# Rows of y in freed weight slots, a list entry from two wide comparisons, the next router's weights in the middle of the expert stage, splits and loads ahead of the branch

## The chip, the cores and the metric

One core of a Trainium2 chip runs the whole program: TensorE (PE), VectorE (DVE), ScalarE (ACT), GpSimd (POOL) and SyncE (SP), which issues most DMAs, in the order written for its queue. The metric is device microseconds of one execution, the median of several.

## The reference

Two decoder layers over 1024 tokens of width 1024, in float32. Layer 0 mixes tokens with a causal convolution module, layer 1 with HGRN2 (a gated linear recurrence, 8 heads of 128). After either mixer comes a hierarchical mixture of experts:

```python
grp_val, grp_idx = top1(softmax(h @ grp_w + grp_b))        # 4 groups
top_val, top_idx = top2(logits of the 8 experts of that group)
gate = grp_val * softmax(top_val)                          # two (token, expert) pairs a token
y = (silu(x @ w_gate[e]) * (x @ w_up[e])) @ w_down[e]      # blocks of at most 128 rows of one expert
h = h + sum of the token's two y, each times its gate
```

There are 32 experts with three matrices of 1024 x 512, 6 MB for one expert. Each sublayer takes its input through an RMS norm, and a last norm ends the trunk.

## The kernel before

Every float32 matmul is made of three: an operand is split into a high half (ScalarE copies it into the matmul format, `wh`) and a low half (VectorE subtracts, `wl`), and high x high, low x high, high x low are summed in PSUM (lines 228 to 240, 680 to 694).

**The expert stage** (`moe`, lines 521 to 946) runs twice. The router's last part (`route`, lines 366 to 455) makes on VectorE a table `tidx` of the rows of each expert; `counts` (line 607) and lines 798 to 801 make `nvt`, the number of further blocks of 128 rows that experts with over 128 rows need. All engines load it and take a branch (lines 802 and 803). Its body (lines 804 to 826) loops over blocks beyond those planned, and is skipped on these inputs. Behind it stand 32 blocks, one an expert, and in layer 0 one listed block more. A block needs six chunks of weights of 1 MB (gate, up, down, two each), each split in two halves; a half is prepared three halves ahead of its matmuls (`prepare`, line 780), over four buffers. Chunks go round twelve slots in layer 0: four of `ring`, two of `ring3`, two of `ring4`, four of `keep`. The first eight are loaded before the stage, the others when a slot is free, in SP's order. A block's rows are gathered by GpSimd (`gather`, line 665), turned on TensorE and split (`x_T`), and its results scattered to `yD` (line 670). The last expert's rows stay on the chip: a one-hot matrix `place` (`places_of`, line 945) spreads them over the tokens with a matmul (`with_last`, line 954).

The extra block of layer 0 is listed on the chip: `entry` (line 733) compares the place of every pair with the block's first place, tile by tile: sixteen compares on VectorE into two buffers of 128 x 128, and a small matmul behind each (lines 744 to 749). It is called after block 19 of the loop, and its sums are read by lines 554 to 566.

**The order.** The instructions of one basic block are ordered for each engine by a planner that simulates a timeline; an instruction may be placed well ahead of where it is written, when its operands are free. `InOrder` keeps the order of TensorE, VectorE and ScalarE for the instructions inside it. `tc.issue_after(x)` lets what it holds stand behind x on x's engine, without a wait. So `places_of`, written at the end of the stage, and `load_router(1)`, written after it, ran ahead of the first branch.

**From the experts to HGRN** (lines 1259 to 1318). `fetch` loads h (8 tiles) into the slots of `keep`, two tiles of y into `ring`, and the first two chunks of HGRN's input weights. `read0` reads the two y rows of 128 tokens (1 MB). For each of eight tiles: y's two rows are added (tile 0 on VectorE, the others on GpSimd, line 1304), h and the last expert's rows are summed in PSUM (`with_last`), VectorE adds y, the norm follows, and TensorE turns the tile and the halves are split (`rows_T`). Tiles 2 to 7 of y go into four buffers `my`, whose memory comes free when the expert stage ends; so tiles 6 and 7 wait until tiles 2 and 3 have been turned. Then come the projections of head 0 (`proj_T` for q and f, by halves of the tokens, and `proj_rows`, by tiles), and the heads one after the other: while one head's recurrence runs, the next one's projections fill TensorE.

Of the kernel before, what the change touches and what calls it, by code (L numbers as in the profile page):

```python
# [13 lines left out]
OP = mybir.AluOpType  # L14
# [25 lines left out]
YB = 4  # L40
# [19 lines left out]
YDVE = (0,)  # L60
# [19 lines left out]
def trunk(ctx, tc, x, conv_norm_w, conv_pw1_w, conv_pw1_b, conv_dw_w, conv_dw_b, conv_ln_g, conv_ln_b,  # L80
# [27 lines left out]
    wides = [None]  # L108

    def load_w(ap3, pool=None):  # L110
        t = (pool or ring).tile([P, WIDE if pool is wides[0] else 2048], F32, name="wraw")[:, :2048]
        v = t if len(ap3.shape) == 2 else t.rearrange("p (a b) -> p a b", a=ap3.shape[1])
        nc.sync.dma_start(v, ap3)
        return t
# [56 lines left out]
    def load_router(l):  # L171
# [10 lines left out]
        nc.vector.tensor_tensor(rw, rw, fcol[:, :, None].to_broadcast([P, KD, 36]), op=OP.mult)  # L182
        r = {"rw": rw, "rb": rb, "lg": const.tile([P, NT, 36], F32, name="lgall"),
# [44 lines left out]
    def split_half(pool, raw, i):  # L228

        hi = pool.tile([P, 1024], F32R, name="wh", bufs=WB)  # L230
        lo = pool.tile([P, 1024], F32R, name="wl", bufs=WB)
# [5 lines left out]
    def split(pool, raw):  # L237

        for i in range(2):
            yield split_half(pool, raw, i)  # L240
# [280 lines left out]
    def moe(l, router, raws, slots, after, last=None, kept=None):  # L521
# [3 lines left out]
        with ExitStack() as held:  # L525
# [6 lines left out]
            over = ring2  # L532
# [163 lines left out]
            def mm_in(ps, xt, raw, c):  # L696
                for z, w in enumerate(split(mp, raw)):
                    done = mm_half(ps, xt, w, 4 * c + 2 * z)
                return done
# [24 lines left out]
            def mm_down(pd, ht, raw, c):  # L724
                for z, w in enumerate(split(mp, raw)):
                    mm_down_half(pd, ht, w, 2 * c + z)

# [5 lines left out]
            def entry(i, tag):  # L733
# [10 lines left out]
                for s in range(2):  # L744
                    for j in range(NT):
                        pl1 = mp.tile([P, P], BF, name="pl1")
                        nc.vector.tensor_scalar(pl1, iota_r, rel[:, s, j:j + 1], None, op0=OP.is_equal)
                        nc.tensor.matmul(tb[:, 0:6], pl1, qv[:, s, j], start=(s == 0 and j == 0),
# [31 lines left out]
            def prepare(n):  # L780
                if n >= len(seq):
                    return
# [4 lines left out]
                with inorder:  # L787
                    ready[n] = split_half(mp, raw_of[key], z)

            gather(xgs[0], cols(0)[0])  # L790
            gather(xgs[1], cols(1)[0])

# [8 lines left out]
            nc.vector.tensor_copy(nvt, nvf)  # L801
            nv = nc.values_load(nvt[0:1, 0:1], min_val=0, max_val=NOV)
            with tc.If(nv > nb - NE):
# [4 lines left out]
                list_rest()  # L808
                with tc.For_i(nb - NE, nv, 1) as it:
# [7 lines left out]
                    for c in range(2):  # L817
                        mm_in(opg, oxt, load_w(moe_src(l, ev, 'g', c), over), c)
                    for c in range(2):
                        mm_in(opu, oxt, load_w(moe_src(l, ev, 'u', c), over), c)  # L820
                    oht = h_T2(h_T(opg, opu))
                    opd = pp.tile([P, D], F32, name="pd", bufs=3 - PGB)
                    for c in range(2):
                        mm_down(opd, oht, load_w(moe_src(l, ev, 'd', c), over), c)
# [24 lines left out]
            for n, (i, part, c, z) in enumerate(seq):  # L849
# [48 lines left out]
                if s_ == 11 or (i == 0 and s_ == 7):  # L898
# [3 lines left out]
                    if i == 4 and l == 0:  # L902
# [4 lines left out]
                                     pp.tile([P, 16], F32, name="tp"))  # L907
                    if i == 20 and nb > NE:
# [16 lines left out]
            left = after(mp)  # L925
# [50 lines left out]
    ring3 = apool("ring30", 2)  # L976
    ring4 = apool("ring40", 2)
    wides[0] = ring4
    with tc.tile_pool(name="convo", bufs=1) as co_pool:
# [10 lines left out]
        with tc.tile_pool(name="a1", bufs=2) as ap, tc.tile_pool(name="a1ps", bufs=2, space=PSUM) as pp:  # L990
# [144 lines left out]
            for n, c in enumerate(ORDER):  # L1135
                if n == 3:
                    router = load_router(0)
# [571 lines left out]
```

## Time and profile before

| | |
|---|---|
| median of three runs | 2361.22 us (2357.2 to 2363.15) |
| profiled execution | 2353.6 us, of which the span 2351.8 |
| PE, DVE, ACT, POOL busy | 95%, 78%, 62%, 22% of the span |
| DMA in the expert stages | some 380 GB/s, share near 1.00 |
| expert stage of layer 0 | about 452 to 1067 us |
| HGRN | about 1067 to 1700 us |
| expert stage of layer 1 | about 1733 to 2320 us |

The page's strip of granted TensorE clock reads 9 in most of its 40 slices and less around 440 us, 1060 us and 1720 us: there one stage gives way to the next. TensorE's busy share of 95% is a mean over stages; the idle time lies in few places. A tile's name in the trace is that of the program (`wl<-wraw,wh`), and "L234" is line 234 of the kernel before.

### The profile page before, as it was taken

How to read it: one execution, taken by the hardware profiler on the slowest of the kernel's cores; microseconds unless marked ns; L12 is line 12 of the kernel's file. 1: busy time of each engine (PE TensorE's matmuls, PEld its weight loads, DVE VectorE, ACT ScalarE, POOL GpSimd, SP SyncE). 2: the span in 40 equal slices, each digit the busy share in tenths (PEclk: the TensorE clock that was granted, in tenths of full speed). 3: DMA queues.
4: the chain of work that ended last, by engine and by line, in shares of the span. 5: the costliest groups of instructions: out<-in, count | busy, mean ns of one | idle time of the engine just before them, and what ended most of it. 6: DMA issues, size and time to landing. Idle time of an engine off the chain costs nothing. (4 is left out here: it accounts for less than half of the span.)

```text
span 2351.8 us, 31895 instructions
## 1 busy us (share of the span) xinstructions
PE 2226.2 (95%) x11825; PEld 1863.3 (79%) x11825; DVE 1842.5 (78%) x2517; ACT 1458.1 (62%) x2035; POOL 511.8 (22%) x310
## 2 busy tenths in 40 slices
PE   7999899699999999998899999989979999999997
PEld 5888777578888878875899999977758888888885
DVE  5898656599999989997376666673479999999996
ACT  5654245378888878884334343332348888888884
POOL 1997301322111111103000000020051111111104
PEclk9999899799999999999999999989979999999999
DMA  5212424499999999987202020205259999999985
GB/s 169 72 55 73 135 90 144 154 338 359 373 377 373 394 354 388 397 323 252 72 14 77 10 82 26 65 32 208 84 201 366 378 374 384 392 391 398 383 329 230
DMA packets 138019, 547.68 MB, mean 233 GB/s; under 512 B 28969, under 2 KB 61921, under 8 KB 87936
## 3 DMA queue, kind: packets, MB, share of 16 engines
q1 hardware_dynamic: 116720, 504.22, 57.5%
q0 software_dynamic: 18720, 33.60, 3.9%
q10 hardware_dynamic: 2416, 7.75, 0.9%
q8 instruction: 95, 1.56, 0.3%
q14 instruction: 68, 0.56, 0.1%
HBM read 519.66 MB, written 60.42 MB: 247 GB/s over the span
## 5 line engine op out<-in xcount | busy, mean ns | idle before, releaser
L234 DVE TENSOR_TENSOR wl<-wraw,wh 128x1024 fp32r<-128x1024 f32 x780 | 932.7, 1229 | 80.6 <-ACT wh L233 71.1
L233 ACT ACTIVATE wh<-wraw 128x1024 fp32r<-128x1024 f32 x780 | 804.3, 1056 | 93.2 <-PE pd L722 77.3
L692 PE MATMUL pu<-wh,xh 128*128 128x512 f32 x520 | 214.6, 413 | 0.0
L692 PE MATMUL pg<-wh,xh 128*128 128x512 f32 x520 | 210.6, 405 | 2.1 <-ACT xh L270 2.1
L692 PE MATMUL pg<-wl,xh 128*128 128x512 f32 x520 | 207.0, 398 | 2.4 <-DVE wl L234 2.2
L692 PE MATMUL pg<-wh,xl 128*128 128x512 f32 x520 | 206.2, 397 | 2.0 <-DVE xl L271 1.9
L720 PE MATMUL pd<-wh,hth 128*128 128x512 f32 x520 | 205.2, 395 | 2.7 <-ACT hth L270 2.7
L692 PE MATMUL pu<-wh,xl 128*128 128x512 f32 x520 | 205.5, 395 | 0.0
L721 PE MATMUL pd<-wl,hth 128*128 128x512 f32 x520 | 204.8, 394 | 0.8 <-DVE wl L234 0.6
L722 PE MATMUL pd<-wh,htl 128*128 128x512 f32 x520 | 204.4, 393 | 0.8 <-DVE htl L271 0.8
L692 PE MATMUL pu<-wl,xh 128*128 128x512 f32 x520 | 203.9, 392 | 0.0
L666 POOL DMA_INDIRECT xg<-xD,tidx x64 | 99.8, 1560 | 463.7 <-PE tp L314 417.5
L671 POOL DMA_INDIRECT yD<-y,yidx x64 | 82.9, 1295 | 497.9 <-ACT y L730 490.2
L1074 POOL TENSOR_TENSOR wraw<-wraw,tap 128x1024 f32<-128x1024 f32 x60 | 155.0, 2584 | 40.5 <-ACT tap L1073 36.1
L1365 PE MATMUL pa<-wih,xh 128*128 128x256 f32 x512 | 147.8, 289 | 5.8 <-ACT q L1346 4.5
L1365 PE MATMUL pa<-wil,xh 128*128 128x256 f32 x512 | 147.6, 288 | 0.0
L1365 PE MATMUL pa<-wih,xl 128*128 128x256 f32 x512 | 147.5, 288 | 0.0
L270 ACT ACTIVATE xh<-tp 128x512 fp32r<-128x512 f32 x146 | 87.0, 598 | 74.3 <-PE tp L314 74.1
L692 PEld LDWEIGHTS pg<-wl,xh 128*128 128x128 f32 x520 | 99.2, 191 | 25.1 <-DVE wl L234 6.8
L692 PEld LDWEIGHTS pg<-wh,xl 128*128 128x128 f32 x520 | 98.8, 190 | 24.3 <-DVE xl L271 3.8
L720 PEld LDWEIGHTS pd<-wh,hth 128*128 128x128 f32 x520 | 98.6, 190 | 23.9 <-ACT hth L270 3.5
L721 PEld LDWEIGHTS pd<-wl,hth 128*128 128x128 f32 x520 | 98.5, 190 | 23.8 <-DVE wl L234 3.0
(492 smaller groups left out, 4874.5 us busy)
## 6 DMA issues: line engine op xcount, KB each, us to landing
wraw<-in_moe_w_gate_dram SPq DMA_DIRECT2D x130, 1024.0 KB, 7.5
wraw<-in_moe_w_up_dram SPq DMA_DIRECT2D x130, 1024.0 KB, 7.6
wraw<-in_moe_w_down_dram SPq DMA_DIRECT2D x130, 1024.0 KB, 7.4
wraw<-in_hgrn_w_in_dram SPq DMA_DIRECT2D x16, 1024.0 KB, 6.6
wraw<-in_conv_pw_w_dram SPq DMA_DIRECT2D x12, 1024.0 KB, 7.0
wraw<-yD SPq DMA_DIRECT2D x10, 1024.0 KB, 9.1
xD<-xn SPq DMA_DIRECT2D x16, 512.0 KB, 2.6
my<-yD SPq DMA_DIRECT2D x6, 1024.0 KB, 6.5
```

The source lines that it names most:

```text
L233: nc.scalar.activation(hi, r, AF.Copy)
L234: nc.vector.tensor_tensor(lo, r, hi, op=OP.subtract)
L270: turned[1] = nc.scalar.activation(hi, ps, AF.Copy)
L666: return nc.gpsimd.indirect_dma_start(out=xg, out_offset=None, in_=xD[l][:, :], in_offset=bass.IndirectOffsetOnAxis(ap=idx, axis=0), bound ...
L671: s = nc.gpsimd.indirect_dma_start(out=yD[l][:, :], out_offset=bass.IndirectOffsetOnAxis(ap=idx, axis=0), in_=y, in_offset=None, bounds_ch ...
L692: done = nc.tensor.matmul(ps, x_[:, kk + k], w_[:, k], start=(kk + k == 0 and x_ is xh and w_ is wh), stop=(kk + k == KD - 1 and x_ is xl))
L720: nc.tensor.matmul(pd[:, ns], hh[:, kk], wh[:, ns], start=(kk == 0), stop=False)
L721: nc.tensor.matmul(pd[:, ns], hh[:, kk], wl[:, ns], start=False, stop=False)
L722: turned[0] = nc.tensor.matmul(pd[:, ns], hl[:, kk], wh[:, ns], start=False, stop=(kk == KF - 1))
L1074: nc.gpsimd.tensor_tensor(res[c], res[c], t, op=OP.add)
L1365: nc.tensor.matmul(pa[:, :256], x_[:, k, js], w_[:, k].rearrange("p z c -> p (z c)"), start=(k == 0 and w_ is wh and x_ is xh), stop=(k == ...
```

## The change

- `entry`: for each of the two slots one compare makes the one-hot rows of all eight tiles (one buffer of 128 x 8 x 128); the sixteen matmuls stay.
- `load_router` is cut in two. `router_weights(1)` (five DMAs and the scaling of `rw`) is written behind block 15's end in the first expert stage, behind the last load on SP.
- The first two halves are split in two steps: `split_hi` (ScalarE) ahead of the count and the branch, `split_lo` (VectorE) behind it, around the turning of the first rows.
- In layer 0 the four loads that follow the first eight are issued ahead of the branch, each waiting for `nvt`.
- `after` (`fetch`, `places_of`) stands, on VectorE, behind the last split of hidden rows.
- `ring3` and `ring4` lie on the other side of the memory and live until HGRN's rows are made. The y tiles 0, 1 and 4, 5 go into `ring4`, 2, 3 and 6, 7 into `ring3`; the `my` buffers are gone. SP's order is h, y 0 and 1, two weight chunks, y 2 and 3, and in the loop y j+4 behind tile j, the other two chunks behind y 5, and the stores of h at the end. All y adds are on GpSimd.
- The weights of head 0 are split, on VectorE, behind the third tile; its projections run q and f of the first half, q and f of the second, then all rows.
- The overflow loop (not entered) loads half chunks into buffers of its own.

```diff
+    def split_hi(pool, raw, i, bufs=WB):
+        hi = pool.tile([P, 1024], F32R, name="wh", bufs=bufs)
+        lo = pool.tile([P, 1024], F32R, name="wl", bufs=bufs)
+        r = raw[:, i * 1024:(i + 1) * 1024]
+        nc.scalar.activation(hi, r, AF.Copy)
+        return hi, lo, r
+    def split_lo(hi, lo, r):
+        nc.vector.tensor_tensor(lo, r, hi, op=OP.subtract)
+        return hi, lo
...
                 for s in range(2):
+                    pl1 = mp.tile([P, NT, P], BF, name="pl1", bufs=1)
+                    nc.vector.tensor_tensor(pl1, iota_r[:, None, :].to_broadcast([P, NT, P]),
+                                            rel[:, s, :, None].to_broadcast([P, NT, P]), op=OP.is_equal)
                     for j in range(NT):
-                        pl1 = mp.tile([P, P], BF, name="pl1")
-                        nc.vector.tensor_scalar(pl1, iota_r, rel[:, s, j:j + 1], None, op0=OP.is_equal)
-                        nc.tensor.matmul(tb[:, 0:6], pl1, qv[:, s, j], ...
+                        nc.tensor.matmul(tb[:, 0:6], pl1[:, j], qv[:, s, j], ...
...
             gather(xgs[0], cols(0)[0])
             gather(xgs[1], cols(1)[0])
+            parts = [split_hi(mp, *raw_half(n)) for n in range(LEAD - 1)]
...
+            nvd = nc.vector.tensor_copy(nvt, nvf)
+            for key in moe_chunks(l)[len(raws):len(raws) + (NRING if l == 0 else 0)]:
+                early[key] = load_w(moe_src(l, *key), slots[order[key] % len(slots)])
+                tc.add_manual_dep(loads[0].ins, nvd.ins.name, ... Sync ...)
             nv = nc.values_load(nvt[0:1, 0:1], min_val=0, max_val=NOV)
             with tc.If(nv > nb - NE):
...
-            for n in range(LEAD - 1):
-                prepare(n)
             with inorder:
+                ready[0] = split_lo(*parts[0])
                 xt[0] = x_T(xgs[0])
+                ready[1] = split_lo(*parts[1])
             prepare(LEAD - 1)
...
+                    if i == 16 and mid:
+                        mid()
...
-            left = after(mp)
+            with tc.issue_after(turned[2].ins):
+                left = after(mp)
...
-        ys = [ring.tile([P, 2048], F32, name="wraw") for _ in range(2)]
-        raws = [in_chunk(0, z) for z in range(2)]
-        for j, y in enumerate(ys):
-            read0(y, j)
+        ys = [read0(ring4, j) for j in range(2)]
+        raws = in_chunks(0, range(2))
+        with tc.issue_after(loads[0].ins):
+            ys += [read0(ring3, j) for j in range(2, 4)]
...
+    def next_router():
+        with tc.issue_after(loads[0].ins):
+            later.extend(router_weights(1))
...
-                (nc.vector if j in YDVE else nc.gpsimd).tensor_tensor(y0, y0, y1, op=OP.add)
+                nc.gpsimd.tensor_tensor(y0, y0, y1, op=OP.add)
...
+                if j == 2:
+                    third = turned[2]
+                if j + 4 < NT:
+                    with tc.issue_after(loads[0].ins):
+                        ys.append(read0(ring3 if j > 1 else ring4, j + 4))
+                if j == 1:
+                    raws += in_chunks(0, range(2, 4))
...
-            ready = projections(weights(0), first_out, [(0,), (1,)])
+            ready = projections(weights(0, third), first_out, ((0, 0), (1, 0), (0, 1), (1, 1)))
```

## Rows read from the trace of the kernel before

**Rows 1.** Busy time by stretches: PE, PEld, DVE, ACT, POOL (count), PE clock, DMA share, GB/s.

```profile
980.00:1000.00 20.00, 20.00 (x95) 16.70 (x94) 18.83 (x19) 17.03 (x20) 3.08 (x3) 1.00 1.01 382
...
1067.00:1078.00 11.00, 6.69 (x20) 3.36 (x19) 7.96 (x6) 4.50 (x5) 3.91 (x2) 0.96 0.84 317
1078.00:1101.00 23.00, 21.56 (x82) 13.01 (x82) 20.43 (x31) 12.10 (x26) 6.90 (x3) 0.94 0.58 190
1101.00:1118.00 17.00, 14.92 (x79) 11.92 (x78) 12.01 (x17) 6.84 (x13) 7.20 (x5) 1.00 0.87 311
1118.00:1129.00 11.00, 5.19 (x26) 4.89 (x26) 3.05 (x3) 6.25 (x7) 0.00 (x0) 0.69 0.00 0
```

**Rows 2.** ACT in order of time, line 885: start, us, operation, idle before.

```profile
825.18 0.59 ACT L885 ACTIVATE hh<-pg 128x512 f32<-128x512 f32 x1
844.28 0.59 ACT L885 ACTIVATE hh<-pg 128x512 f32<-128x512 f32 x1
867.65 0.59 ACT L885 ACTIVATE hh<-pg 128x512 f32<-128x512 f32 x1
885.47 0.58 ACT L885 ACTIVATE hh<-pg 128x512 f32<-128x512 f32 x1
```

**Rows 3.** PE in order of time, at the list entry.

```profile
851.53 0.86 PE L314 MATMUL tp<-ident,xg 128*128 128x128 f32 x4 [2.22 <-DVE rowf L556]
```

**Rows 4.** DVE in order of time, ahead of the first branch.

```profile
436.10 0.46 DVE L182 TENSOR_TENSOR rw<-rw,fcol 128x288 f32<-128x288 f32 x1 [0.89 <-DMA rw<-in_router_exp_w_dram]
...
445.07 1.22 DVE L950 TENSOR_TENSOR place<-iota_r,rel 128x1024 fp32r<-128x1024 f32 x1
...
446.62 0.15 DVE L801 CAST nvt<-nvf 128x1 int32<-128x1 f32 x1
```

**Rows 5.** PE in order of time, start of the first expert stage.

```profile
451.99 1.94 PE L314 MATMUL tp<-ident,xg 128*128 128x128 f32 x8 [7.82 <-DVEq L803]
456.08 0.79 PE L692 MATMUL pg<-wh,xh 128*128 128x512 f32 x1 [2.15 <-ACT xh L270]
```

**Rows 6.** ACT in order of time, same place.

```profile
453.32 2.00 ACT L233 ACTIVATE wh<-wraw 128x1024 fp32r<-128x1024 f32 x2
```

**Rows 7.** PE in order of time, start of the second expert stage.

```profile
1733.31 1.94 PE L314 MATMUL tp<-ident,xg 128*128 128x128 f32 x8 [6.82 <-DMA xg<-xD,tidx]
1735.09 0.79 PE L692 MATMUL pg<-wh,xh 128*128 128x512 f32 x1
...
1737.03 0.79 PE L692 MATMUL pg<-wh,xl 128*128 128x512 f32 x1 [0.73 <-DVE xl L271]
```

**Rows 8.** Line 803, the branch, both stages: ns, first and last start us.

```profile
L803 DVEq EVENT_SEMAPHORE  x2: 21/21/21, 451.9 to 1729.0; - x2
```

**Rows 9.** Tile xg, 440 to 475 us: the gathers, issue to landing.

```profile
DMA to landing us min/median/max: 4.3/5.0/8.1
```

**Rows 10.** SP in order of time, reads of y for tiles 2 to 7.

```profile
1067.37 2.19 SPq L1276 DMA_DIRECT2D my<-yD  x4
...
1096.66 3.88 SPq L1276 DMA_DIRECT2D my<-yD  x2
```

**Rows 11.** DVE in order of time, from the experts to HGRN.

```profile
1068.76 1.28 DVE L935 SCALAR_TENSOR_TENSOR xl<-pd,gates,xh 128x1024 fp32r<-128x1024 f32 x1 [6.26 <-ACT xh L934]
...
1073.50 3.38 DVE L1304 TENSOR_TENSOR wraw<-wraw 128x1024 f32<-128x1024 f32 x1
...
1080.01 3.08 DVE L298 SCALAR_TENSOR_TENSOR wraw<-wraw,ss,nw 128x1024 f32<-128x1024 f32 x1
...
1102.40 0.69 DVE L271 TENSOR_TENSOR xl<-sc,xh 128x512 fp32r<-128x512 f32 x1 [0.78 <-ACT xh L270]
...
1118.67 0.69 DVE L271 TENSOR_TENSOR xl<-sc,xh 128x512 fp32r<-128x512 f32 x1 [0.78 <-ACT xh L270]
```

**Rows 12.** PE in order of time, first row projection of head 0.

```profile
1122.49 0.58 PE L1365 MATMUL pa<-wih,xh 128*128 128x256 f32 x1 [4.48 <-ACT q L1346]
```

**Rows 13.** PE in order of time, late in the second expert stage.

```profile
2286.08 0.50 PE L721 MATMUL pd<-wl,hth 128*128 128x512 f32 x1 [0.62 <-DVE wl L234]
```

More of the change, by code (lines that the diff above doesn't have):

```diff
@@ L519, in first_chunks, with moe @@
         return [load_w(moe_src(l, *keys[i]), pool) for i, pool in enumerate(pools)]
-    def moe(l, router, raws, slots, after, last=None, kept=None):
+    def moe(l, router, raws, slots, after, last=None, kept=None, mid=None):
         with ExitStack() as held:
@@ L694, in mm_half, with over_half @@
                 return done
[L696 to L699, printed above, removed]
+            def over_half(ev, part, i):
+                raw = ring2.tile([P, 2048], F32, name="wraw")[:, :1024] if NRING2[l] else \
+                    rp.tile([P, 1024], F32, name="oraw", bufs=1)
+                nc.sync.dma_start(raw, moe_src(l, ev, part, i // 2)[:, i % 2 * 1024:(i % 2 + 1) * 1024])
+                return split_lo(*split_hi(rp, raw, 0, 1))
             def h_T(pg, pu, name="hh"):
@@ L800, in moe @@
             nc.vector.tensor_reduce(nvf, past.rearrange("p b e -> p (b e)"), axis=AX.X, op=OP.add)
-            nc.vector.tensor_copy(nvt, nvf)
+            nvd = nc.vector.tensor_copy(nvt, nvf)
+            for key in moe_chunks(l)[len(raws):len(raws) + (NRING if l == 0 else 0)]:
+                early[key] = load_w(moe_src(l, *key), slots[order[key] % len(slots)])
+                tc.add_manual_dep(loads[0].ins, nvd.ins.name, mybir.DependencyInfo(
+                    mybir.DependencyClass.Sync, mybir.DependencyReason.DATA), reason="behind the rows")
             nv = nc.values_load(nvt[0:1, 0:1], min_val=0, max_val=NOV)
@@ L808, in moe @@
                 list_rest()
+                rp.release()
+                rp = apool(f"over{l}", 1)
                 with tc.For_i(nb - NE, nv, 1) as it:
@@ L975, in trunk @@
     zD = dram.tile([P, npe, CW], F32, name="zD")
-    ring3 = apool("ring30", 2)
-    ring4 = apool("ring40", 2)
+    ring3 = apool("ring30", 2, side="right")
+    ring4 = apool("ring40", 2, side="right")
     wides[0] = ring4
@@ L1136, in trunk @@
                 if n == 3:
[L1137 removed]
+                    router = load_router(0, *router_weights(0))
                 if n % 2 == 0 and n:
@@ L1312, in trunk @@
                 rows.append(h)
-            with tc.issue_after(loaded.ins):
+                if j == 2:
+                    third = turned[2]
+                if j + 4 < NT:
+                    with tc.issue_after(loads[0].ins):
+                        ys.append(read0(ring3 if j > 1 else ring4, j + 4))
+                if j == 1:
+                    raws += in_chunks(0, range(2, 4))
+            with tc.issue_after(loads[0].ins):
                 for j, h in enumerate(rows):
                     nc.sync.dma_start(rD[j * P:(j + 1) * P, :], h)
-        bi = apool("b1i", 1)
         kept.release()
         keep.release()
+        ring4.release()
+        ring3.release()
+        bi = apool("b1i", 1)
         hp_ = apool("b2", 1, side="right")
```

89 lines of the change are left out of this document (37 added, 52 removed).

## The prediction

> **What bounds the kernel.** I read the busy table by stretches first, then who waits on whom, then the order of single engines around each gap. In the middle of either expert stage TensorE is busy without a break at a granted clock of 1.00, while VectorE works 18.83 of 20 us [rows 1]; ScalarE's activation of each block recurs every 17.82 us [rows 2]. So a block is bound by TensorE, and nothing saved on another engine inside such a block shows at the end. What can be won lies where TensorE stands still or runs at half clock: at the list entry (block 21), at the start of either expert stage, between the first expert stage and the HGRN heads, and briefly before the end. All work behind each of these places hangs on TensorE's order, so a microsecond taken out there is a microsecond at the end. The sums are made against the profiled execution, 2353.6 us (span 2351.8 and 1.8 around it); the median of the three timed runs, 2361.2, is 7.6 above it, and I carry the difference in us over to that median.
>
> **1. List entry: 5.0 us off.** The two periods that hold it are 19.10 and 23.37 us against 17.82 [rows 2]: 1.28 + 5.55 = 6.8 us. Inside stands a gap of 2.22 us ahead of a transpose [rows 3]: sixteen compares and sixteen matmuls take turns over two small buffers, and the splits that TensorE needs queue behind them on VectorE. Now there are two compares over all eight tiles, with the shape of the `place` compare, 1.22 us each [rows 4], so one turn is left instead of fourteen. The sixteen matmuls stay; I keep 1.8 us for them and for the second compare in VectorE's queue. Bounds: 1 us (the gap stays, since the single large buffer makes the second compare wait for eight matmuls) to 6.5.
>
> **2. Start of the first expert stage: 3.5 us off.** VectorE's chain up to the count `nvt` (446.77) decides when the branch is taken. Two foreign instructions stand in it: scaling the next router's weights, 0.89 waiting for its DMA and 0.46 of work, and `place`, 1.22 [rows 4]. One moves to block 16, the other behind the last split of the stage: 2.4 us earlier (the two overlap their neighbours by 0.1 to 0.2), and the gather of the first rows 1.3 earlier. Behind the branch, TensorE's first expert matmul comes 4.09 us after its first transpose, 456.08 against 451.99 [rows 5], since ScalarE makes two 1 us halves first [rows 6]; the second stage, where the rows arrive later than those halves are done, shows what the path needs without them: 1735.09 against 1733.31, 1.78 us [rows 7]. With the halves ahead of the branch that is 2.3 us. Together 4.7 at best, and some 0.7 more if a wait for `xl` as in the second stage [rows 7] goes too.
> Against it stands what is now issued ahead of the branch: four loads of 1 MB on SP (4 MB, 10.5 us at 382 GB/s [rows 1]), with 2 us of issuing before SP reads the count. They bring TensorE nothing, for eight chunks are loaded already and last 24 us. But the first gather then shares the DMA engines: it landed 4.3 to 8.1 us after issue, the longest being the one issued beside the weights [rows 9]; issued 1.3 earlier and landing 3 to 4 later, it would undo the earlier branch. VectorE's release at the branch is the other exposed piece: 451.9 in the first stage, over 4 us after its compare, against 1729.0 and half a microsecond in the second [rows 8]; whatever held it could take longer beside 4 MB. Bounds: 5.4 off to 5 added (the release delayed by the whole 10.5); I take 3.5, nearer the side of the sum, since the loads are issued only after the count.
> On this the Trainium skill, Runtime: NRT & Kernel Launch, "Instruction fetch mechanics", speaks against the change: a taken branch to code outside the two pages at hand must fetch it by DMA. By that rule the 4 us would be such a fetch, and the four loads would delay it; rival C is worked out for it from rows. The trace neither bears it out nor refutes it: the page of the profile counts instruction queues among the DMA, but no row says which engine they served.
>
> **3. Start of the second expert stage: 0.9 off.** The gather binds here (6.82 us idle until it lands), and stays; no load is added. The wait of 0.73 for `xl` goes, since VectorE makes the first low half before the rows arrive [rows 7], and a little of the next half. Bounds 0 to 2.
>
> **4. From the experts to HGRN: 12 us off.** From 1067 to 1129 TensorE is idle 4.31 + 1.44 + 2.08 + 5.81 = 13.6 us [rows 1], and about 3 more go to the lower of its two clocks, 1.2 instead of 2.4 GHz (granted 0.94 from 1078 on, 0.69 from 1118 on). More than 16.7 cannot be won. The chain is VectorE's: per tile of rows two adds out of PSUM, a scaling, two splits. From the end of its first add (1076.88) to the sixth tile's last split (1103.09) it takes 26.2 us, 4.37 per tile; then it waits for the last two reads, issued only at 1096.66, for want of a slot, and the eighth tile ends at 1119.36 [rows 10, 11]. After the change the reads of tiles 0 to 3 go into slots of finished weights, before the last matmuls end, and tiles 4 to 7 follow as tiles 0 to 3 are turned. The first add of y, 3.38 us on VectorE at 1073.50, goes to GpSimd; the weight splits stand behind the third tile. So VectorE begins at about 1071 (right after `yl`, 1068.76 + 1.28, and the first sums), and eight tiles at 4.37 plus two weight splits (2.4, at the 1.22 of `place`) end at 1108.4. The DMA path says the same: the last read is issued when the fourth tile is turned, about 1089; from the last read before (1100.5, the end of the SP row) to the last split took 18.8 us, so 1108. Behind 2 MB of weights it may be 2 or 3 later. I take 1109.5: 9.9 us earlier. After it TensorE now waits until 1122.49, then again, for ScalarE's q and f, behind table changes and two splits [rows 12]; as the q and f projections of both halves now come ahead of the row projections, the second half needs only one of these: 2 to 2.5 us less. New waits are small: q and f of the first head now lie where rows of h lay, so their evictions wait for the stores of those rows; the last is issued at about 1102 and lands ahead of 1110.
> What speaks against it: eight GpSimd adds instead of seven, all beside VectorE. The scaling took 3.08 us at 1080.01, beside such an add, against 1.28 for `yl`, the same form of instruction [rows 11]; of the six tiles in the pace only one was so hit. If six more are, at 1.8 each less the one counted, 9 us come back. Bounds: 3 to 16.
> By the Trainium skill, SBUF — State Buffer, "Who interferes with whom", a VectorE instruction with two SBUF inputs and a GpSimd one that reads SBUF exclude each other for the whole instruction, whichever starts first. The trace agrees for the scaling (3.08 us) and, in its sense, for the add of y (3.38); by the rule every overlap would cost, which is rival A.
>
> **5. Before the end: 0.8 off.** `place` of the second stage held up a split, and TensorE waited 0.62 for it [rows 13] and a little at the next half. It now runs behind the last hidden-row split, where VectorE has nothing until the last block's matmuls end. Bounds 0 to 1.
>
> **Edits at nothing.** The router weights in block 16: 0.46 us of VectorE, covered by its 1.1 us of slack per block (1.17 of 20 [rows 1]); five DMAs of small pieces on SP, covered by the chunks loaded ahead; if VectorE meets them before they have landed it stands still, with everything behind it on its queue (the splits), about 5 us at the worst. The overflow loop is not entered. hD's loads keep their place, and the two w_in loads behind the y reads are wanted late.
>
> **Sum:** 5.0 + 3.5 + 0.9 + 12 + 0.8 = 22.2 us: 2331.4 for a profiled execution, **2339** for the median.
>
> **Rivals.** A: the transition gives most back, through the exclusion above or the reads of the last two tiles behind weights and stores; its gain is 3 instead of 12: 2348. For it: both slow rows of VectorE; against: the adds of the first two tiles now fall before the chain begins. B: the orders that a planner writes change little at the branch and the entry (it moved `place` and the router ahead of the branch in the first place), so both bring 1 or less: 2346.5. Against: both now have edges that forbid it. C: the loads delay the branch; start 5 us later instead of 3.5 earlier: 2347.5. For: the release of 4 us; against: little of it is known to be DMA. D, the other side: VectorE, with 1.1 us of slack per block, loses its pace in the expert blocks because the planner's new order puts low halves later; from 0.34 us per block over 65 blocks the whole gain is gone, at 0.5 it is 32 us added: 2371. For it: the block with extra VectorE work took 23.37. Against: nothing is added per block, and the split halves keep their ordered chain.
>
> **How the numbers follow.** Forecast 0.58 (2331 to 2346 of its own); A 0.13, C 0.09, B 0.06, two of these at once 0.07 (some 2355); D 0.07. A change under 0.3%, 7 us, can't be told from none. Faster than 2354: 0.58 + 0.13 + 0.09 + 0.06 = 0.86; same 0.07, two rivals at once; slower 0.07, D. The range, 2329 to 2354, leaves out one tenth below and the doubled rivals and D above.
>
> **What would show it.** Right: periods around block 21 of 19.5 us or less; `nvt` 2.4 us earlier after the last logits and TensorE's first expert matmul under 2 us behind the first transpose; last tile's split before 1111, counted from a stage end at 1067.4; less than 6 us idle from there to the row projections. Wrong: VectorE's scalings at 3 us in most tiles; the gather landing after 8 us, or VectorE's release after 5; blocks longer than 17.82. The forecast falls if the transition brings under 6 us or the blocks lengthen.

## The result: 0.7% slower, and the profile after

The kernel after takes **2376.91 us** (median of five runs, 2374.34 to 2378.04) against 2358.26 beside it (five runs, 2356.25 to 2363.15): ratio 1.0074, interval 1.0059 to 1.0088. 2339 was forecast, 2329 to 2354 as the range, and slower had a chance of 0.07. The profiled executions differ by 24.0 us of span (2351.8 and 2375.8), 5.4 more than the medians: the profiled execution before, 2353.6 us, was quicker than all five runs beside the result, and where in the span that lies is not known. Cut at points that both traces have, those 24 us stand as follows; the last column is what the five steps put into the same stretch.

| stretch | before | after | difference | forecast |
|---|---|---|---|---|
| start to the last router logits | 433.60 | 435.29 | +1.7 | 0 |
| last logits to `nvt` | 13.02 | 10.70 | -2.3 | -2.4 |
| `nvt` to the third block's first `hh` | 55.39 | 68.27 | +12.9 | -1.1 |
| from there to the end of expert stage 1 | 565.17 | 568.43 | +3.3 | -5.0 |
| end of stage 1 to `nvt` of stage 2 | 660.67 | 658.56 | -2.1 | -12.0 |
| `nvt` to the third block's first `hh` | 51.67 | 53.80 | +2.1 | -0.9 |
| from there to the end | 572.28 | 580.75 | +8.5 | -0.8 |

Three rows carry it: the start of stage 1, and the two long rows of plain blocks. First the place that went as forecast, ScalarE's activations round block 21 (start, duration, operation):

```profile
824.27 0.59 ACT L894 ACTIVATE hh<-pg 128x512 f32<-128x512 f32 x1
842.45 0.59 ACT L894 ACTIVATE hh<-pg 128x512 f32<-128x512 f32 x1
861.22 0.58 ACT L894 ACTIVATE hh<-pg 128x512 f32<-128x512 f32 x1
879.41 0.59 ACT L894 ACTIVATE hh<-pg 128x512 f32<-128x512 f32 x1
```

The two periods that hold the entry, 19.10 and 23.37 us [rows 2], are 18.18 (first to second) and 18.77 now: 5.5 us less, and TensorE no longer stops. But the plain period behind them is 18.19, where it was 17.82. The stretches say why it can't be another engine's wait (columns as in [rows 1]):

```profile
840.00:860.00 20.00, 20.00 (x107) 16.12 (x106) 18.93 (x28) 16.28 (x19) 3.46 (x2) 1.00 1.02 372
980.00:1000.00 20.00, 20.00 (x93) 16.38 (x92) 18.48 (x19) 16.61 (x19) 2.61 (x2) 1.00 1.00 377
```

TensorE is busy for 20.00 of 20 at a granted clock of 1.00, as before [rows 1], yet 93 matmuls fall into the stretch where 95 did (741 against 756 from 880 to 1040 us), and VectorE and ScalarE did less, not more. Each matmul starts later behind the one ahead of it. One group of three in the down projection, before:

```profile
929.06 0.39 PE L720 MATMUL pd<-wh,hth 128*128 128x512 f32 x1
929.29 0.39 PE L721 MATMUL pd<-wl,hth 128*128 128x512 f32 x1
929.52 0.39 PE L722 MATMUL pd<-wh,htl 128*128 128x512 f32 x1
929.74 0.39 PE L720 MATMUL pd<-wh,hth 128*128 128x512 f32 x1
```

and after:

```profile
923.86 0.39 PE L722 MATMUL pd<-wh,hth 128*128 128x512 f32 x1
924.09 0.40 PE L723 MATMUL pd<-wl,hth 128*128 128x512 f32 x1
924.33 0.39 PE L724 MATMUL pd<-wh,htl 128*128 128x512 f32 x1
924.56 0.39 PE L722 MATMUL pd<-wh,hth 128*128 128x512 f32 x1
```

Read the starts, not the durations: from one `wh`,`hth` matmul to the next it was 0.68 us and is 0.70. With no wait, and every engine's order in a block the same, the period went from 17.82 to 18.17; over 52 undisturbed periods that is some 18.5 us.

The other loss, at the start of stage 1, stands first on VectorE (in brackets the idle time before, and what ended it):

```profile
445.99 0.15 DVE L804 CAST nvt<-nvf 128x1 int32<-128x1 f32 x1
446.06 1.22 DVE L240 TENSOR_TENSOR wl<-wraw,wh 128x1024 fp32r<-128x1024 f32 x1
461.44 0.19 DVE L571 TENSOR_TENSOR ex<-lgall,small 128x32 f32<-128x32 f32 x1 [14.16 <-SPq L811]
...
479.45 0.20 DVE L650 TENSOR_SCALAR qv<-tok 128x16 bf16<-128x16 f32 x1 [7.64 <-POOL qv L648]
```

and in TensorE's order:

```profile
455.65 1.94 PE L315 MATMUL tp<-ident,xg 128*128 128x128 f32 x8 [11.02 <-DMA xg<-xD,tidx]
463.93 0.79 PE L692 MATMUL pg<-wh,xh 128*128 128x512 f32 x1 [6.34 <-ACT xh L271]
...
480.98 0.79 PE L692 MATMUL pu<-wl,xh 128*128 128x512 f32 x1 [5.18 <-DVE wl L240]
```

VectorE goes on behind the branch 15.3 us after `nvt` has ended, where it was about 5. The rows have been gathered and transposed by then, but their splits wait for ScalarE and VectorE behind the branch, so the first expert matmul comes 8.3 us after the first transpose, not 2.3. Then VectorE stands 7.64 us for GpSimd, which is late too, and holds up the next low half.

### The profile page after: what moved, and what is told of

The parts are those of the page before. It is cut to its first block, busy times and chain, and to the rows that moved or that the text cites. A ratio compares the mean times of both kernels' runs of the same rounds, so it can differ in the third digit from the quotient of the medians.

```text
span 2375.8 us, 31866 instructions
## 1 busy us (share of the span) xinstructions
PE 2241.3 (94%) x11825; PEld 1862.0 (78%) x11825; DVE 1842.2 (78%) x2502; ACT 1457.7 (61%) x2035; POOL 508.7 (21%) x311
## 3 DMA queue, kind: packets, MB, share of 16 engines
q8 instruction: 95, 1.56, 0.3%
## 5 line engine op out<-in xcount | busy, mean ns | idle before, releaser
L692 PEld LDWEIGHTS pg<-wh,xh 128*128 128x128 f32 x520 | 99.5, 191 | 29.3 <-ACT xh L271 7.0
L724 PEld LDWEIGHTS pd<-wh,htl 128*128 128x128 f32 x520 | 97.9, 188 | 25.0 <-DVE htl L272 2.1
```

Source lines behind the costliest of these rows:

```text
L692: done = nc.tensor.matmul(ps, x_[:, kk + k], w_[:, k], start=(kk + k == 0 and x_ is xh and w_ is wh), stop=(kk + k == KD - 1 and x_ is xl))
L724: turned[0] = nc.tensor.matmul(pd[:, ns], hl[:, kk], wh[:, ns], start=False, stop=(kk == KF - 1))
```

## Experiments

Two questions: what stretches the matmuls, and what holds the branch. The first had a theory at once. `parts`, made ahead of the branch, takes the split halves `wh` and `wl` out of the pool ahead of `xh`, `xl` and some small tiles, so all these addresses move. By the compiled program's allocation `wh` of stage 1 lay at 129504 and `xh` at 113120, and they lie at 65856 and 114144 now. Theory: this placement sets the matmuls' spacing (at first, the start of the moving tile `wh` modulo 64 bytes, which was 32 and is 0 now). Of a matmul's two operands the tile with 512 columns (`wh`, `wl`) is called moving, the one of 128 by 128 (`xh`, `xl`, `hth`, `htl`) stationary. Rivals: the new order of ScalarE's and VectorE's work does it, or the loads. A few bytes of pad move addresses and leave the orders alone.

**e1_after_half32** and **e2_before_at64** shift the halves by 32 bytes, in the kernel after and in the one before:

```
+ mp.tile([P, 8], F32, name="pada", bufs=1)   # 32 bytes
  parts = [split_hi(mp, *raw_half(n)) for n in range(LEAD - 1)]
+ mp.tile([P, 8], F32, name="padb", bufs=1)
```

(in the kernel before the same two pads stand round the first `wh` and `wl` of the stage).

> The changed kernel with 32 unused bytes ahead of the split weight tiles and 32 behind them, so that wh and wl start at 32 past a multiple of 64 bytes again, as in the kernel before; every other tile keeps its offset modulo 64, every engine its order. Theory A (TensorE's pace follows the start of the moving tile modulo 64): the period of an expert block falls from 18.17 back to 17.82 us, the three matmuls of one row group from 0.70 to 0.68 us, and 60 periods at 0.355 give 21 us: 2377 to about 2356. Rival B (the pace comes from what else the change moved: the tiles lie in another part of SBUF, or the neighbours on the other engines): the period stays at 18.17 and the time at 2377.

> The kernel before with the same two pads around its weight tiles: wh and wl start at a multiple of 64 bytes, all else keeps its offset modulo 64, the order of every engine is that of the kernel before. Theory A: periods of 18.17 instead of 17.82, about 21 us slower, 2379. Rival B: 17.82 and 2358.

e1: 2362.89, ratio 1.0030 (1.0013 to 1.0048), period 17.92. e2: 2374.55, 1.0089 (1.0071 to 1.0107), period 18.16: 64 bytes of unused memory (two pads of 32) make the kernel before as slow as the changed one. The order and the loads are out as causes of the pace; placement it is.

**e3_after_all64** takes only the second pad.

> The changed kernel with one pad of 32 bytes behind the weight tiles only: wh and wl (moving) stay at a multiple of 64 and the stationary tiles xh, xl, hth, htl come to a multiple of 64 too. Theory A1 (the start of the moving tile alone decides): period 18.17, time 2377. Theory A2 (it is the difference between moving and stationary tile modulo 64): 17.82, some 2356. Rival B: 18.17, so it is told from A1 by the first run only.

2360.60, ratio 1.0018 (1.0006 to 1.0031), period 17.90. The halves lie where they lay in the changed kernel and the pace is nearly back; so it isn't the start of the moving tile by itself. The start of the stationary tile, or its distance to the moving one, is left; the runs further down tell these apart.

**e4_loads_early** and **e10_one_load** turn to the branch. The loop that issues four loads behind the count issues none, or one (in e4 the planner puts all four ahead of the count, in e10 the other three come behind the branch):

```
- for key in moe_chunks(l)[len(raws):len(raws) + (NRING if l == 0 else 0)]:
+ for key in moe_chunks(l)[len(raws):len(raws) + (0)]:   # e10: (1 if l == 0 else 0)
```

> The changed kernel without the loop that loads four weight chunks behind the count nvt and ahead of the branch; the planner puts these four loads among the stores of the last token rows instead, some 15 us before the count, so that they have landed when the branch is taken. Theory L (the four loads in flight hold up the release at the branch): VectorE and GpSimd are released at 450 to 453 us instead of 461.4, the stage starts 8 to 10 us earlier, and with the start's second stall (VectorE waits 7.6 us for GpSimd's zeroed qv) unchanged the time is 2367 to 2370. Rival M (the release is late because the code behind the branch changed, loads or not): release still at 459 or later, time 2375 to 2378. The block period stays at 18.17 in both.

> The changed kernel with one weight chunk instead of four behind the count and ahead of the branch (1 MB instead of 4); the other three are loaded behind the branch. Theory L (the release waits until the loads in flight are through; 1.2 us with none, 15.3 with four): release at 4 to 6 us behind the count nvt, the stage starts 9 to 11 us earlier than with four. Rival Q (one load in SP's queue between the count and the branch is enough, whatever its size): release 10 us or more behind the count. The period stays at 18.17 and the time is 2365 to 2370 by L, 2374 or more by Q.

VectorE in e4:

```profile
443.08 0.15 DVE L804 CAST nvt<-nvf 128x1 int32<-128x1 f32 x1
...
445.14 0.19 DVE L571 TENSOR_TENSOR ex<-lgall,small 128x32 f32<-128x32 f32 x1 [0.77 <-SPq L811]
```

and in e10:

```profile
444.78 0.15 DVE L804 CAST nvt<-nvf 128x1 int32<-128x1 f32 x1
...
450.90 0.19 DVE L571 TENSOR_TENSOR ex<-lgall,small 128x32 f32<-128x32 f32 x1 [4.83 <-SPq L811]
```

From the end of `nvt` to the release: 1.9 us with no load, 6.0 with one, 15.3 with four. The traces show what VectorE waits for, too. Behind the branch SP has nine semaphore instructions, each waiting for one semaphore, and VectorE and GpSimd wait for SP. Their first and last starts in the kernel before (L803), in e4, in e10 and in the changed kernel (L811):

```profile
L803 SPq EVENT_SEMAPHORE  x9: 17/17/17, 447.8 to 448.4; - x9
L811 SPq EVENT_SEMAPHORE  x9: 17/17/17, 444.3 to 444.9; - x9
L811 SPq EVENT_SEMAPHORE  x9: 17/17/17, 446.4 to 450.7; - x9
L811 SPq EVENT_SEMAPHORE  x9: 17/17/17, 449.4 to 461.2; - x9
```

In the changed kernel four of the nine wait for the semaphores that the four loads raise when they land, and go on at 451.4, 455.2, 458.4 and 460.9. The last load, issued at 447.55, lands at 460.9:

```profile
DMA to landing us min/median/max: 13.4/13.4/13.4
```

So the release waits until SP has seen every load land. The 5 us of the kernel before are something else, as VectorE's own first instruction behind the branch shows, before and after:

```profile
L803 DVEq EVENT_SEMAPHORE  x1: 21/21/21, 451.9 to 451.9; - x1
L811 DVEq EVENT_SEMAPHORE  x1: 21/21/21, 447.4 to 447.4; - x1
```

Before, SP was through at 448.4 and VectorE itself came at 451.9; what held it isn't shown. In the changed kernel it was there at 447.4 and then stood for SP. The time is 2364.82 (1.0049, 1.0032 to 1.0066) and 2370.81 (1.0060, 1.0040 to 1.0079). In e4 the first `hh` comes 17.00 us after `nvt` (30.58 in the changed kernel, 21.58 before), but the second 36.16 (49.04; 36.20): against the kernel before, the lead is gone one block later, where VectorE stands 4.1 us for GpSimd's `qv`.

**e5_early_pad128** is e4 with pads of 32 and 96 bytes, which bring moving and stationary tiles to a distance of 0 again, modulo 256.

> The kernel with the four loads ahead of the count (the run before with early loads), and pads of 32 and 96 bytes around wh and wl: moving and stationary tiles of the experts now start at the same offset modulo 128 (both at 96), as in the kernel before. Theory P128 (the pace follows the difference modulo 128: 0 gives 17.82, 64 gives 17.9, 32 or 96 gives 18.17): period 17.82 and, with 60 periods at 0.355, 2365 - 21 = 2344. Rival P64 (only the difference modulo 64 counts and the 0.08 left over is something else): 17.90 to 17.92, time 2348. If pace and loads do not add up, the time is above 2352.

2341.55, ratio 0.9945 (0.9929 to 0.9962), period 17.83. With pace and branch mended the change is 0.55% faster than the kernel before.

**e6_early_pad_slots** adds to e5 the two slots that the transition lacks: six reads of y before the first turn, as before, two of them in `ring` (and its second pad has 864 bytes, a distance of 0 as well). **e7_early_pad_gate** is e5, leaves the slots at four and issues the gate table's matmuls six half chunks later, with `qv` zeroed ahead of the branch.

```
+ y23 = [ring.tile([P, 2048], F32, name="wraw") for _ in range(2)]      # e6
...
+ ys += [read0(y23[j - 2], j) for j in range(2, 4)]
+ ys += [read0(ring3, j) for j in range(4, 6)]
...
- if i == 1 and s_ == 3:                                               # e7
+ if i == 0 and s_ == 9:
```

> The same with a pad of 864 instead of 96 bytes (the difference is then 0 modulo 2048, as in the kernel before), and six slots instead of four for the rows of y between the first expert stage and HGRN: tiles 2 and 3 go into the general weight ring, 4 and 5 into the slots of the last block's down weights, 6 and 7 into those of tiles 0 and 1; the second pair of w_in loads waits for tiles 2 and 3. Theory S (step 4 failed because a read of y waits until the tile four places ahead is turned): the last tile's low half comes 4 to 9 us earlier counted from the end of the last block, and the time is 4 to 8 us under that of the run without the slots, about 2338. Rival V (the chain on VectorE and ScalarE sets the pace, slots or not): no more than 1.5 us gained. Period: 17.82 if a difference of 0 modulo 2048 is needed and 96 bytes of pad did not give it; the same as in the run with 96 bytes otherwise.

> The early loads and the pads of 32 and 96 bytes, and the sixteen matmuls of the gate table put six half chunks later in TensorE's order (into the down projection of block 0 instead of the gate projection of block 1), the zeroing of qv by GpSimd ahead of the branch. Theory G (the losses of the second block of stage one and the third block of stage two are waits for GpSimd, which builds the gate table): the second period of stage one falls from 19.2 to under 16 us and the third of stage two from 23.4 to under 20, together 5 to 8 us: about 2337 against 2344. Rival T (they come from VectorE, which makes many low halves in one run and is late with the rest): the two periods stay within 1.5 us and the time at 2343 or more.

e6: 2345.34 (0.9954, 0.9938 to 0.9971), no faster than e5. From the end of stage 1 to the last head's `q` 439.86 us, 4.9 less than in e5, as expected, but the third period of stage 2 rose from 25.01 to 28.86. There GpSimd issues the gather of block 2 at 1747.38, behind 22 operations of the gate table and 32.0 us after `nvt`, as in e5; but now TensorE waits for the rows (why they land later isn't shown):

```profile
1754.98 0.68 PE L315 MATMUL tp<-ident,xg 128*128 128x128 f32 x4 [2.23 <-DMA xg<-xD,tidx]
```

e7: 2343.49 (0.9941, 0.9918 to 0.9964), no faster than e5 either. Stage 1's second `hh` comes 32.0 us after `nvt`, not 36.9, but in stage 2 the same wait is worse:

```profile
1753.04 1.09 PE L315 MATMUL tp<-ident,xg 128*128 128x128 f32 x4 [6.78 <-DMA xg<-xD,tidx]
```

The half that concerns stage 1 held, the half for stage 2 fell: it needs the gather ahead of the masks.

**e8_all** joins e5, e6 and e7, and issues the second half of the masks behind block 2's gather.

```
+ with tc.issue_after(first["g"].ins) if before and s else ExitStack():
      nc.gpsimd.tensor_scalar(pl[:, s, j], iota_r, rank[:, s, j:j + 1], None, op0=OP.is_equal)
```

> Everything that helped in one kernel: early loads, pads (moving and stationary tiles 0 modulo 2048 apart), six slots for the rows of y, qv zeroed ahead of the branch, the gate table's matmuls six half chunks later, and new: the second half of the gate table's masks on GpSimd stands behind the gather of block 2. Theory G (behind the branch GpSimd's queue is the bound: with TensorE starting earlier the gather of block 2, queued behind the masks, lands too late): TensorE's wait for that gather in stage two (2.2 and 6.8 us in the two runs before) goes, the third period of stage two falls from 25 to 28.9 to under 21.5 us, and the time to 2331 to 2336. Rival R (TensorE starts earlier than the weights come, and the period stays above 24 whatever stands first in GpSimd's queue): 2340 or more. Faster than the kernel before in both, by 18 to 24 or by some 14 us.

**2332.68 us**, ratio 0.9895 (0.9879 to 0.9910, before at 2358.89): 1% faster than the kernel before. The third period of stage 2 is 20.99 (TensorE still waits 1.9 us for block 2's rows), and `nvt` to the third `hh` 49.66 (51.67 before).

**e9_x_off32**, **e13_x_off32_h0**, **e11_h_off32** and **e14_off128** are e8 with pads that set the distance of `xh`, `xl` and of `hth`, `htl` apart; **e12_one_pad96** is the changed kernel with one pad of 96 bytes behind the first halves.

```
+ mp.tile([P, 8], F32, name="padc", bufs=1)     # e9, e13: once, ahead of the first xh
+ mp.tile([P, 24], F32, name="padd", bufs=1)    # once, behind the first xl; e13: 56 instead of 24
+ the same two, 8 and 24                        # e11: once, round the first hth and htl
- mp.tile([P, 216], F32, name="padb", bufs=1)   # e14: the pad of e8 behind parts
+ mp.tile([P, 248], F32, name="padb", bufs=1)
+ mp.tile([P, 24], F32, name="padb", bufs=1)    # e12: behind parts
```

> The kernel with everything that helped, and pads of 32 and 96 bytes around xh and xl alone: these stationary tiles start at 0 modulo 128, 96 bytes off the moving tiles (wh, wl at 96), while hth and htl, the stationary tiles of the down projection, stay at 96. Theory A2 (each matmul's pace is set by its own two operands' difference): the triples of the gate and up projections take 0.70 us, those of the down projection 0.68; the period is 18.0 to 18.1, about 12 us more in all, 2344 to 2347. Rival N (the pace belongs to some other pair, as the tiles that VectorE or ScalarE writes meanwhile, or to hth and htl): all three kinds at one pace, period 17.83 (2333) or 18.17 (2351).

> The kernel with everything that helped, and pads of 32 and 96 bytes around hth and htl alone (stationary in the down projection): they start at 0 modulo 128, 96 off the weight tiles; xh and xl stay level with the weights. Shifting xh and xl alone has slowed all three projections alike, so a matmul's own pair does not explain it. Theory X (one pace for the whole block, and the tiles of the 48 gate and up matmuls set it): period 17.83, time 2333. Theory Y (one pace for the block, and any stationary tile that is an odd multiple of 32 bytes off the weights slows it): 18.17 in all three, time about 2351. Theory A2 as first put (each matmul by its own pair): triples of the down projection 0.70, the others 0.68, period 17.93 to 18.0, some 2340.

> The changed kernel with nothing but one pad of 96 bytes behind the weight tiles: moving and stationary tiles all start at 64 modulo 128 (a difference of 0 at another absolute offset than in the kernel before, where it is 96). Theory D (the difference decides, not the offset): period 17.83, 2377 - 20 = 2356 to 2358. Rival O (96 modulo 128 is needed): 17.9 to 18.17, 2361 to 2377.

> As the run with xh and xl off by 32, but with a pad of 224 instead of 96 bytes behind them: hth and htl are level with the weights modulo 256 and not only modulo 128. Theory M256 (each matmul is paced by its own pair, and the offset counts modulo 256): triples of the gate and up projections 0.70, of the down projection 0.68, period 18.0 to 18.1 instead of 18.17. Rival M128 (modulo 128 counts, and the x tiles set one pace for the block): 0.70 everywhere, 18.17.

> The kernel with everything that helped, and a pad larger by 128 bytes behind the weight tiles: all stationary tiles lie 128 off the moving ones modulo 256 (level modulo 128). Theory M256: triples of 0.70 (or 0.69), period 18.0 to 18.17, about 2345 to 2351. Rival M128: 0.68, 17.83, 2333.

Start of the stationary tile less that of the moving one, modulo 256, against the spacing of three matmuls and the period:

| run | `xh`, `xl` | `hth`, `htl` | three of pg, pu | three of pd | period us | time us |
|---|---|---|---|---|---|---|
| before; e5 to e8; e12 | 0 | 0 | 0.68 | 0.68 | 17.79 to 17.84 | 2332.7 to 2358.3 |
| e1, e3 | 192 | 192 | 0.687 | 0.687 | 17.92, 17.90 | 2362.89, 2360.60 |
| after; e4 | 160 | 160 | 0.70 | 0.70 | 18.17 | 2376.91; 2364.82 |
| e2 | 224 | 32 | 0.70 | 0.70 | 18.16 | 2374.55 |
| e9 | 32 | 128 | 0.70 | 0.70 | 18.17 | 2352.08 |
| e14 | 128 | 128 | 0.70 | 0.70 | 18.15 | 2353.26 |
| e13 | 32 | 0 | 0.70 | 0.68 | 18.03 | 2347.31 |
| e11 | 0 | 32 | 0.67 to 0.70 | 0.70 | 18.00 | 2346.66 |

Ratios to the kernel before: e9 0.9987 (0.9974 to 0.9999), e11 0.9960 (0.9945 to 0.9976), e12 0.9995 (0.9985 to 1.0005), e13 0.9965 (0.9951 to 0.9979), e14 0.9990 (0.9981 to 1.0000). My first rule, modulo 64, fell with e1 and e3, which were short of the full pace; modulo 128 fell with e9, whose down projection was slow too, its distance being 128. The start of the stationary tile alone falls as well: at 224 modulo 256 it goes with the quick pace in the kernel before and with the slow one in the changed kernel and e14. What is left is the distance modulo 256 (189 times 256 bytes in stage 1 of e5 and e12, a multiple of 2048 in the kernel before, e6 and e8), and each matmul goes by its own pair, as e13 shows on TensorE (down projection, then the next block's gate projection):

```profile
901.86 0.39 PE L724 MATMUL pd<-wh,hth 128*128 128x512 f32 x1
...
905.95 0.39 PE L724 MATMUL pd<-wh,hth 128*128 128x512 f32 x1
...
907.33 0.40 PE L694 MATMUL pg<-wh,xh 128*128 128x512 f32 x1
...
910.13 0.40 PE L694 MATMUL pg<-wh,xh 128*128 128x512 f32 x1
```

The first two stand six groups of three apart, 4.09 us or 0.68 a group; the last two four, 2.80 us or 0.70: two levels within 9 us, on one engine at a granted clock of 1.00. e11's period is 0.06 above what a third of the loss would give (17.94); that stays unexplained. e9 and e11 also lose some 3.5 us in the third period of stage 2 (24.45 and 24.70, against 20.99 in e8), so their times tell less than their periods. And e12 costs a line: 96 bytes, and the changed kernel, branch and transition as they are, is level with the one before.

## Why the prediction was wrong

**What bounds the kernel: held, but a premise under it failed.** "A block is bound by TensorE" is so in both kernels. That its period of 17.82 us therefore stays was never written as a step, and it is the largest term that failed: 18.5 of the 46.2 us between the forecast and the outcome of the profiled executions (37.9 between the medians, 2339 and 2376.91). A bound engine's own speed was taken as fixed. The change part spoke of tiles allocated ahead of the branch only as work. Rival D had the size right (0.34 us per block to undo the gain; measured 0.355) and the cause wrong: VectorE's low halves aren't late, and TensorE doesn't wait.

**Step 1, list entry: right.** 5.5 us off between the activations as they stand, 6.2 against two periods of the new pace; 5.0 forecast, bounds 1 to 6.5. The marker, periods of at most 19.5, is met by both (18.18, 18.77). So rival B, the planner's order unchanged, is out.

**Step 2, start of stage 1: failed.** Its first half held: `nvt` comes 2.3 us sooner after the last logits, 2.4 forecast. The second half was to give 1.1 more and cost 12.9, a gap of 14.0. The doubt was stated (a release "delayed by the whole 10.5") and then priced away by "the loads are issued only after the count": after the count is just when SP reaches the branch, behind which it waits for every load to land, and VectorE and GpSimd wait for SP: 1.9, 6.0, 15.3 us for none, one and four. Rival C had the effect, at 5 where the release alone took 10 more, and GpSimd's late `qv` 3 beyond it; the 4 us of [rows 8] that spoke for it were VectorE's own and have gone. The markers "VectorE's release after 5" and "the gather landing after 8 us" read it rightly (15.3, and 9.5 and 11.3 for the two gathers). The Trainium skill, Runtime: NRT & Kernel Launch, "Instruction fetch mechanics", has a taken branch fetch its target by DMA when it is outside the two pages at hand. The trace doesn't bear this out for the 15.3 us, which end with the landing of the last load; whether it is behind the 4 us of the kernel before, no row shows. The second branch, without loads beside it, releases VectorE 1.5 us after its `nvt` has ended.

**Step 3, start of stage 2: the gain came and was given back.** The first `hh` follows `nvt` 3.2 us sooner (19.58 to 16.35), more than the 0.9 forecast. Two blocks on it is lost: the third period rises from 19.15 to 25.20. GpSimd's masks are late, and TensorE waits for them; GpSimd first:

```profile
1745.03 3.52 POOL L597 TENSOR_SCALAR pl<-iota_r,rank 128x128 bf16<-128x128 f32 x6
1748.72 1.10 POOL L666 DMA_INDIRECT xg<-xD,tidx  x1 [0.17 <-issue]
1749.87 9.37 POOL L597 TENSOR_SCALAR pl<-iota_r,rank 128x128 bf16<-128x128 f32 x6
```

VectorE beside it:

```profile
1749.13 8.49 DVE L240 TENSOR_TENSOR wl<-wraw,wh 128x1024 fp32r<-128x1024 f32 x7
```

and TensorE, in the second and longest of four stops that add up to 3.0 us:

```profile
1771.89 0.26 PE L599 MATMUL pd<-qg,pl 128*128 128x96 bf16 x1 [1.42 <-POOL pl L597]
```

Six masks take 3.52 us beside VectorE's small operations and 9.37 beside seven low halves in a row. That isn't new. The same twelve masks in the kernel before:

```profile
1731.61 5.28 POOL L597 TENSOR_SCALAR pl<-iota_r,rank 128x128 bf16<-128x128 f32 x6
1738.21 6.85 POOL L597 TENSOR_SCALAR pl<-iota_r,rank 128x128 bf16<-128x128 f32 x6
```

They took 12.1 us and take 12.9. New is that TensorE comes to the gate table 27.4 us after `nvt`, where it was 31.3, while GpSimd is done with the masks at 31.7, where it was 29.2: the change brought one engine forward and not the other, which the prediction didn't weigh. And the stops cost more than their 3.0 us. The third period, before and after (columns as in [rows 1]):

```profile
1760.37:1779.52 19.15, 18.84 (x89) 15.42 (x88) 17.32 (x20) 15.22 (x18) 2.79 (x3) 1.00 0.96 347
1769.85:1795.05 25.20, 22.75 (x94) 18.09 (x95) 18.32 (x21) 15.21 (x18) 7.81 (x8) 0.86 0.80 282
```

TensorE stands 2.45 us in it, not 0.31, and its granted clock is 0.86, so for part of it the lower level of 1.2 GHz, worth some 3.5 us by an estimate from these two lines (0.14 of 25.20). In e8 it is 1.00. The Trainium skill, SBUF — State Buffer, "Who interferes with whom", says that a VectorE instruction with two SBUF inputs and a GpSimd one that reads SBUF shut each other out, and the rows agree: 0.59 us a mask against 1.56. The same section says that TensorE waits on nobody; the table of distances shows that this doesn't make its pace a constant, 0.68 against 0.70 with no other engine's order changed.

**Step 4, experts to HGRN: failed, 2 us instead of 12.** The chain per tile was right, the supply wasn't. SP's reads of y (as in [rows 10]) after:

```profile
1068.41 0.88 SPq L1295 DMA_DIRECT2D wraw<-yD  x2
...
1072.38 26.53 SPq L1295 DMA_DIRECT2D wraw<-yD  x4
...
1109.73 6.54 SPq L1295 DMA_DIRECT2D wraw<-yD  x2
```

The freed weight slots are four; before there were six places for y. So reads 5 to 8 stand in SP's queue until a tile has been turned; the last two go out from 1109.73 on, 27 us and more after the end of the stage (1082.69), and the forecast had the last at 22 (1089 against 1067.2). GpSimd's first addition on a late tile waited 11.40 us:

```profile
1101.67 2.36 POOL L1324 TENSOR_TENSOR wraw<-wraw 128x1024 f32<-128x1024 f32 x1 [11.40 <-DMA wraw<-yD]
```

The last split starts at 1142.28, 59.6 us after the end of the stage, where 51.5 was measured before and 41.6 was forecast (1109.5 less 0.69, from 1067.2). The new order of the projections makes that up, by more than the 2 to 2.5 forecast for it: the first `q` comes 53.7 us after the end of the stage, ahead of the last split, where it was 54.7, so the stretch as a whole is 2.1 shorter. TensorE's clock is no better, in the same columns:

```profile
1083.10:1101.00 17.90, 13.75 (x49) 7.86 (x49) 10.45 (x15) 9.66 (x15) 4.75 (x2) 0.95 0.41 152
1101.00:1119.00 18.00, 15.56 (x50) 8.88 (x48) 15.41 (x19) 7.61 (x16) 8.11 (x3) 0.86 0.78 246
1119.00:1129.00 10.00, 8.83 (x38) 7.33 (x39) 7.89 (x11) 3.15 (x7) 2.40 (x1) 0.83 1.02 388
1129.00:1147.00 18.00, 13.96 (x63) 11.10 (x62) 7.68 (x10) 9.75 (x15) 2.47 (x3) 0.91 0.14 56
```

Granted 0.83 to 0.95 throughout, that is, the lower level of 1.2 GHz for part of each stretch. Rival A named the late reads of the last tiles; here it is four reads, not two. Its other half, the exclusion, came in part: of the eight scalings three take 2.25 to 3.19 us, the others 1.28, which adds up to 4.3 us. Two more slots are worth 4.9 us (e6 against e5). Even e8, with 52.1 us to its last split, is 10.5 from the forecast: that rest I haven't explained.

**Step 5, before the end: right.** The last period went from 26.54 to 25.33, 1.2 off against 0.8 forecast.

**Edits at nothing: right.** The router's weights in block 16 find their DMA landed (0.45 us of VectorE, no wait). The 1.7 us before the last logits lie ahead of every place the change touches by intent; no run looked into them.

In sum, by the profiled executions: the pace 18.5, the start of stage 1 14.0, the transition 9.9, stage 2's third block 3.0 and the first stretch 1.7, less about 1 won at entry and end, are the 46.2.

## What to carry to other kernels

Where one engine is busy without a break, check its instructions' spacing, not its busy share, before and after any edit that adds, drops or reorders a tile: an allocation moved for reasons of order can change it by 2 to 3%, and a pad of 96 bytes undo that. Issue no bulk loads just ahead of a branch: here SP waited behind it until each had landed, and other engines waited for SP. Work put ahead of a start is won only if the slowest producer behind it (here GpSimd's masks and gathers) comes forward as well.

## What the runs showed of the hardware that was not expected

- A matmul of 512 columns with a 128 by 128 stationary tile starts every 0.227 us if both SBUF operands begin at the same place modulo 256 bytes, every 0.229 at a distance of 192, and every 0.233 at 32, 128, 160 or 224, all at a granted clock of 1.00 (other distances weren't run). Why 192 costs a third of the others is open.
- Behind this program's branch SP waits for the landing of the loads it has issued, and VectorE's release waits for SP: 1.9, 6.0 and 15.3 us after the count with 0, 1 and 4 MB issued just ahead of the branch.
- GpSimd's 128x128 comparison takes 0.59 us beside small VectorE operations and 1.56 beside a row of VectorE subtractions from SBUF.
